# Turning attention probabilities with a transposing DMA instead of TensorE, in a one-core hybrid streaming layer

## The chip, the cores and the metric

The kernel runs on one core of a Trainium2 chip. The metric is device time in microseconds (us) of one execution. Before the change the median of three runs is 1910.07 us (1909.86 to 1910.68).

## What is computed

One layer of a streaming encoder over 1024 prompt frames and 32 sample frames, with 512 cached frames for the sample part. The part that the change touches is differential attention: eight heads, two softmax maps per head, their difference times the values.

```python
s = jnp.einsum('bqhcd,bkhcd->bhcqk', q_blk, ka).astype(jnp.float32) * scale
mask = k_chunk[None, :] <= q_chunk[:, None]
p = jax.nn.softmax(jnp.where(mask, s, -jnp.inf), axis=-1)
a = p[:, :, 0] - lam * p[:, :, 1]
return jnp.einsum('bhqk,bkhe->bqhe', a.astype(va.dtype), va)
```

Beside it run a retention branch with the same heads, an output projection, a SwiGLU block of width 2816 and a gated per-layer embedding.

## The kernel before

All matrix products of fp32 data are made from fp16 pairs: a number is scaled and split into a head ("hi") and a rest ("lo"), and a product is three fp16 matmuls (hi·hi, hi·lo, lo·hi).

The first stage, from the start to about 1050 us, is the input projection with attention and retention. Its work comes in units: 8 heads times 9 blocks of 128 rows, of which blocks 0 to 7 are the prompt and block 8 is the sample. Each unit is made twice, as `unit_a` (q, k, v and attention) and, four units later, as `unit_b` (retention, gates and the mix). Each begins with a projection of 24 matmuls of 512 columns (lines 734 to 736). Weights come by 1 MB loads on the queue of SyncE (SP), four per head, line 407. The later stages (output projection, gate and up products, down product, the gated embedding) begin behind that.

`attend` is the attention of one unit:

- TensorE makes the scores (lines 875 and 878) into a bank `sc`, one map at a time when there are more than 512 keys.
- VectorE reduces the maximum (line 885), VectorE or GpSimd scales it (line 887), ScalarE takes the exponential with the row sum (line 895) into two SBUF tiles `p` of 1024 fp32 columns. The pool has five of them.
- VectorE joins the two maps (line 909): `p0 = p0 + cz * p1`. Rows are queries, columns are keys.
- For the product with the values the keys have to lie on the partitions. Block i has i + 1 key blocks of 128 columns; the sample unit has five. TensorE turns each 128x128 fp32 block against an identity (line 924), up to four blocks into one PSUM bank `t`. ScalarE or VectorE writes the scaled fp16 head out of the bank (lines 931 and 933), VectorE the rest (line 935), both into the tile `aT` (two buffers).
- TensorE multiplies `aT` with the values (lines 943, 944, 947) into a bank `po`; ScalarE takes it out (line 956).

In all there are 8 x (1 + 2 + ... + 8 + 5) = 328 blocks to turn.

The order of the work is not written by hand. Each unit is a Python generator that announces its next step with an assumed price (`V`, `S`, `G`, `M`, `DM` for VectorE, ScalarE, GpSimd, TensorE and DMA), its waits and the buffers that it takes and gives back. `Flow` plays the generators against each other and emits the instruction that could start first. What it emits is a fixed order on each engine; on the chip an engine waits where an operand is late. `either` lets Flow choose between two engines by their assumed loads. DMAs are issued from SP in the order in which Flow reached them.

Of the kernel before, what the change touches and what calls it, by code (L numbers as in the profile page):

```python
# [11 lines left out]
F32 = mybir.dt.float32  # L12
F16 = mybir.dt.float16
BF16 = mybir.dt.bfloat16
I32 = mybir.dt.int32
AF = mybir.ActivationFunctionType
ALU = mybir.AluOpType
# [4 lines left out]
P = 128  # L22
D = 1024
# [35 lines left out]
def V(n, f=1.0, x=0.0):  # L59
    return {"V": 0.07 + x + f * n / 960.0}  # L60


def S(n, x=0.0):
    return {"S": 0.1 + x + n / 1200.0}
# [6 lines left out]
def M(us):  # L71
    return {"M": us}


def DM(mb):
    return {"D": mb * 2.9}


def either(*ds):
    out = {}  # L80
    for d in ds:
        out.update(d)
    return out
# [100 lines left out]
def kernel(  # L184
# [26 lines left out]
    nc = tc.nc  # L211
# [30 lines left out]
    id32 = cst_sb[:, 0, :]  # L242
# [245 lines left out]
    with ExitStack() as pa:  # L488
# [18 lines left out]
        lsc = ca.tile([P, 1], F32, name="lsc")  # L507
# [5 lines left out]
        wk = pa.enter_context(DT(name="wk", bufs=2))  # L513
# [3 lines left out]
        ps_o = pa.enter_context(DT(name="ps_o", bufs=3, space=PSUM))  # L517
# [346 lines left out]
        def attend(key, i, R, q4, sblocks, masked, vblocks, NK, sc_ap, do_ap):  # L864
            pm, Z = [], sm(2, "Z", 6)
            nm = sm(2, "nm", 6)
            nb = sm(2, "nb", 6)
            for ms in ((0, 1),) if NK <= 512 else ((0,), (1,)):
# [3 lines left out]
                for m in ms:  # L872
                    for b0, n, kts in sblocks:
                        o = ps[0:R, 512 * ms.index(m) + b0:512 * ms.index(m) + b0 + n]
# [11 lines left out]
                g = yield either(V(1, 1.0, 0.06), G(1, 0.2))  # L886
                ENG[g].tensor_scalar(out=nb[0:R, mc], in0=nm[0:R, mc], scalar1=sc_ap[0:R], scalar2=None, op0=ALU.mult)  # L887
                for m in ms:
                    yield ("get", "p")
                    yield S(NK, 0.14)  # L890
                    pt = pp_.tile([P, 1024], F32, tag="p", name="p")
                    if NK % P and not m:
# [13 lines left out]
                                           op0=ALU.mult, op1=ALU.mult)  # L906
            p0, p1 = pm[0][0:R, 0:NK], pm[1][0:R, 0:NK]
            yield V(NK, 1.0, 0.06)
            nc.vector.scalar_tensor_tensor(out=p0, in0=p1, scalar=cz[0:R], in1=p0, op0=ALU.mult, op1=ALU.add)
            yield ("put", "p")  # L910
            yield V(1)
            dz = sm(1, "dz", 6)
            nc.vector.tensor_tensor(out=dz[0:R], in0=rz[0:R, 0:1], in1=do_ap[0:R], op=ALU.mult)
            nb_ = len(vblocks)
            yield ("get", "aT")
            aT = wk.tile([P, 2, 8, P], F16, tag="aT", name="aT")
            for j0 in range(0, nb_, 4):
                js = range(j0, min(j0 + 4, nb_))
                yield ("get", "o")
                yield M(0.107 * len(js))  # L920
                pt = ps_o.tile([P, 512], F32, tag="o", name="t").rearrange("p (b c) -> p b c", b=4)
                for j in js:
                    n = vblocks[j][0]
                    nc.tensor.transpose(out=pt[0:n, j - j0, 0:R], in_=pm[0][0:R, j * P:j * P + n], identity=id32[0:R, 0:R])
                if js[-1] == nb_ - 1:
                    yield ("put", "p")
                n, nj = vblocks[js[-1]][0], len(js)
                hi = aT[0:n, 0, j0:j0 + nj, 0:R]
                g = yield either(S(nj * R, 0.05), V(nj * R, 1.0, 0.06))
                if g == "S":  # L930
                    nc.scalar.activation(hi, pt[0:n, 0:nj, 0:R], AF.Copy, scale=lsc[0:n])
                else:
                    nc.vector.tensor_scalar(out=hi, in0=pt[0:n, 0:nj, 0:R], scalar1=lsc[0:n], scalar2=None, op0=ALU.mult)
                yield V(nj * R, 1.0, 0.06)
                nc.vector.scalar_tensor_tensor(out=aT[0:n, 1, j0:j0 + nj, 0:R], in0=pt[0:n, 0:nj, 0:R], scalar=lsc[0:n], in1=hi,
                                               op0=ALU.mult, op1=ALU.subtract)
                yield ("put", "o")
            yield ("get", "o")
            yield M(0.165 * nb_)
            po = ps_o.tile([P, 512], F32, tag="o", name="po")[0:R, 0:P]  # L940
            for j in range(nb_):
                n, v_hi, v_lo = vblocks[j]
                nc.tensor.matmul(out=po, lhsT=aT[0:n, 0, j, 0:R], rhs=v_hi, start=(j == 0), stop=False)
                nc.tensor.matmul(out=po, lhsT=aT[0:n, 0, j, 0:R], rhs=v_lo, start=False, stop=False)
            for j in range(nb_):
                n, v_hi, v_lo = vblocks[j]
# [4 lines left out]
            if u >= NQ:  # L951
# [13 lines left out]
                                           op0=ALU.mult, op1=ALU.mult)  # L965
# [1123 lines left out]
```

## Time and profile before

| | |
|---|---|
| median of three runs | 1910.07 us |
| span of the profiled execution | 1908.6 us |
| matmuls | 14223 |
| first turn of a probability block (line 924) | at 59.6 us |
| last value product (line 947) | at 1019.0 us |
| granted TensorE clock | 0.998 |

The profiled execution's own time is its span and some 1.5 us around it, if it is taken to be the median. In the profile PE is TensorE's matmuls, PEld its weight loads, DVE is VectorE, ACT is ScalarE, POOL is GpSimd and SP is SyncE, which issues the DMAs. "L924" is line 924. A matmul row's duration runs from its start to a modelled end; matmuls overlap, so the time that one occupies the array is the distance to the next one's start. A wait line reads: who waited, for whom, us in total, times, longest.

### The profile page before, as it was taken

How to read it: one execution, taken by the hardware profiler on the slowest of the kernel's cores; microseconds unless marked ns; L12 is line 12 of the kernel's file. 1: busy time of each engine (PE TensorE's matmuls, PEld its weight loads, DVE VectorE, ACT ScalarE, POOL GpSimd, SP SyncE). 2: the span in 40 equal slices, each digit the busy share in tenths (PEclk: the TensorE clock that was granted, in tenths of full speed). 3: DMA queues.
4: the chain of work that ended last, by engine and by line, in shares of the span. 5: the costliest groups of instructions: out<-in, count | busy, mean ns of one | idle time of the engine just before them, and what ended most of it. 6: DMA issues, size and time to landing. Idle time of an engine off the chain costs nothing.

```text
span 1908.6 us, 38365 instructions
## 1 busy us (share of the span) xinstructions
PE 1859.8 (97%) x14223; PEld 1220.3 (64%) x14223; DVE 1497.7 (78%) x3940; ACT 1087.3 (57%) x2842; POOL 680.9 (36%) x1149
## 2 busy tenths in 40 slices
PE   7999999999999999999999997999999999999999
PEld 3556565555655566655556685777777776666666
DVE  7888888788787787777887589999999986654364
ACT  7777677677676776766666345655555552101132
POOL 3654444445444544544442067333232300000010
PEclk9999999999999999999999999999999999999999
DMA  5222112112021121211215610222211116112031
GB/s 194 70 72 78 60 32 82 36 55 83 24 70 58 50 64 34 79 59 31 85 33 187 226 65 31 101 86 83 69 55 66 47 54 262 61 62 79 10 133 50
DMA packets 71949, 146.90 MB, mean 77 GB/s; under 512 B 25265, under 2 KB 52145, under 8 KB 63826
## 3 DMA queue, kind: packets, MB, share of 16 engines
q1 hardware_dynamic: 71762, 144.46, 22.7%
q8 instruction: 111, 1.82, 0.4%
q14 instruction: 76, 0.62, 0.1%
HBM read 113.09 MB, written 31.34 MB: 76 GB/s over the span
## 4 chain that ended last, share of the span: by engine, by line
PE 73%; DVE 12%; POOL 7%; ACT 5%; issue 2%; DMA 1%; SPq 0%; POOLq 0%; ACTq 0%; DVEq 0%
PE ps L474 10%; PE ps L475 10%; PE ps L476 10%; PE pj L734 7%; PE pj L736 7%; PE pj L735 7%; PE ps L1478 4%; PE ps L1477 4%; PE ps L1476 4%; ACT p L895 2%; DVE nm L885 2%; DVE w L467 1%; POOL qkr L770 1%; PE sc L875 1%; PE sc L878 1%
## 5 line engine op out<-in xcount | busy, mean ns | idle before, releaser
L734 PE MATMUL pj<-w,xh 128*128 128x512 f16 x1024 | 389.0, 380 | 2.8 <-ACT w L465 2.8
L735 PE MATMUL pj<-w,xh 128*128 128x512 f16 x1024 | 389.0, 380 | 0.6 <-DVE w L467 0.6
L736 PE MATMUL pj<-w,xh 128*128 128x512 f16 x1024 | 389.0, 380 | 0.0
L475 PE MATMUL ps<-mixs,w 128*128 128x352 f16 (+1 forms) x960 | 260.4, 276 | 5.9 <-DVE mixs L1501 5.9
L474 PE MATMUL ps<-mixs,w 128*128 128x352 f16 (+1 forms) x960 | 260.4, 276 | 0.3 <-ACT pws L1354 0.3
L476 PE MATMUL ps<-mixs,w 128*128 128x352 f16 (+1 forms) x960 | 260.5, 276 | 0.0
L476 PEld LDWEIGHTS <-w 128*128 128x128 f16 x1736 | 170.4, 98 | 56.2 <-issue 6.0
L474 PEld LDWEIGHTS <-w 128*128 128x128 f16 x1736 | 170.6, 98 | 54.4 <-issue 4.4
L475 PEld LDWEIGHTS <-w 128*128 128x128 f16 x1736 | 170.4, 98 | 49.8 <-issue 1.6
L736 PEld LDWEIGHTS <-xh 128*128 128x128 f16 x1024 | 100.3, 98 | 122.3 <-issue 1.9
L1634 POOL TENSOR_TENSOR st<-st 128x512 f32<-128x512 f32 x66 | 88.2, 1336 | 244.7 <-DVE w L1629 186.6
L734 PEld LDWEIGHTS <-xh 128*128 128x128 f16 x1024 | 101.3, 99 | 76.7 <-issue 3.7
L735 PEld LDWEIGHTS <-xh 128*128 128x128 f16 x1024 | 100.2, 98 | 74.6 <-issue 3.7
L895 ACT ACTIVATE p<-sc,nb,scs 128x256 f32<-128x256 f32 (+7 forms) x128 | 106.4, 832 | 71.5 <-POOL nb L887 49.0
L474 PE MATMUL ps<-tT,w 128*128 128x352 f16 (+1 forms) x528 | 144.0, 277 | 0.0
L475 PE MATMUL ps<-tT,w 128*128 128x352 f16 (+1 forms) x528 | 143.9, 277 | 0.0
L476 PE MATMUL ps<-tT,w 128*128 128x352 f16 (+1 forms) x528 | 143.8, 277 | 0.0
L1629 DVE SCALAR_TENSOR_TENSOR w<-st,gus,w 128x512 f16<-128x512 f32 x132 | 141.4, 1072 | 0.1
L885 DVE TENSOR_REDUCE nm<-sc 128x2 f32<-128x256 f32 (+6 forms) x112 | 102.7, 917 | 19.7 <-PE sc L878 18.4
L1478 PE MATMUL ps<-a,w 128*128 128x352 f16 x312 | 97.5, 313 | 0.5 <-DVE w L1720 0.5
L1477 PE MATMUL ps<-a,w 128*128 128x352 f16 x312 | 97.5, 313 | 0.0
L1476 PE MATMUL ps<-a,w 128*128 128x352 f16 x312 | 97.5, 313 | 0.0
(432 smaller groups left out, 4861.1 us busy)
## 6 DMA issues: line engine op xcount, KB each, us to landing
st<-in_win_dram SPq DMA_DIRECT2D x30, 1024.0 KB, 4.9
st<-in_wgu_dram SPq DMA_DIRECT2D x22, 1024.0 KB, 4.8
st<-in_wdn_dram SPq DMA_DIRECT2D x16, 704.0 KB, 4.7
out_dram<-kv SPq DMA_DIRECT2D x64, 128.0 KB, 1.7
a_d<-a SPq DMA_DIRECT2D x9, 528.0 KB, 2.6
b<-a_d SPq DMA_DIRECT2D x9, 528.0 KB, 7.5
mixs<-mix_d SPq DMA_DIRECT2D x8, 528.0 KB, 6.1
pw_d<-pws SPq DMA_DIRECT2D x12, 352.0 KB, 5.3
```

What stands on the lines that cost most here:

```text
L474: nc.tensor.matmul(out=ps, lhsT=wh, rhs=ah, start=first, stop=False)
L475: nc.tensor.matmul(out=ps, lhsT=wh, rhs=al, start=False, stop=False)
L476: nc.tensor.matmul(out=ps, lhsT=wl, rhs=ah, start=False, stop=last)
L734: nc.tensor.matmul(out=ps, lhsT=xhi, rhs=w[:, k, 0], start=(k == 0), stop=False)
L735: nc.tensor.matmul(out=ps, lhsT=xhi, rhs=w[:, k, 1], start=False, stop=False)
L736: nc.tensor.matmul(out=ps, lhsT=xh[:, k, 1, t0:t0 + P], rhs=w[:, k, 0], start=False, stop=(k == KD - 1))
L885: nc.vector.tensor_reduce(out=nm[0:R, mc], in_=pv, axis=AX.X, op=ALU.max, negate=True)
L895: nc.scalar.activation(pt[0:R, 0:NK], ps[0:R, p0:p0 + NK], AF.Exp, bias=nb[0:R, m:m + 1], scale=sc_ap[0:R], accum_out=Z[0:R, m:m + 1])
L1476: nc.tensor.matmul(out=ps, lhsT=wt[:, 0, j], rhs=a[:, 0, cs], start=(first and j == js[0]), stop=False)
L1477: nc.tensor.matmul(out=ps, lhsT=wt[:, 1, j], rhs=a[:, 0, cs], start=False, stop=False)
L1478: nc.tensor.matmul(out=ps, lhsT=wt[:, 2, j], rhs=a[:, 1, cs], start=False, stop=(last and j == js[-1]))
L1629: nc.vector.scalar_tensor_tensor(out=w[:, i, 1], in0=src, scalar=s, in1=w[:, i, 0], op0=ALU.mult, op1=ALU.subtract)
```

## The change

The turn by TensorE is taken out. After the two maps are joined, head and rest are made in rows in SBUF: the second `p` tile, whose content is used up, is viewed as 2048 fp16 columns and takes the head of all key blocks and behind it the rest. Each is one instruction over all key blocks, where before there was one for each four blocks. One transposing DMA, issued from SP, then turns all of it into `aT`. The value product is as before, and waits for the DMA. In Flow the DMA has the assumed price `xbar` on the DMA resource and lands after the delay `landed`; the second `p` tile is given back when it has landed, the first as soon as the rest is made.

```diff
+def xbar(tiles):
+    return 0.5 + 0.027 * tiles
+def landed(tiles):
+    return ("delay", 2.0 + 0.03 * tiles)
...
-            yield ("put", "p")
             yield V(1)
             dz = sm(1, "dz", 6)
             nc.vector.tensor_tensor(out=dz[0:R], in0=rz[0:R, 0:1], in1=do_ap[0:R], op=ALU.mult)
             nb_ = len(vblocks)
+            NB = nb_ * P
+            pf = pm[1].bitcast(F16)
+            hi, lo, src = pf[0:R, 0:NB], pf[0:R, NB:2 * NB], pm[0][0:R, 0:NB]
+            g = yield either(S(NB, 0.05), V(NB, 1.0, 0.06))
+            if g == "S":
+                nc.scalar.activation(hi, src, AF.Copy, scale=lsc[0:R])
+            else:
+                nc.vector.tensor_scalar(out=hi, in0=src, scalar1=lsc[0:R], scalar2=None, op0=ALU.mult)
+            yield V(NB, 1.0, 0.06)
+            nc.vector.scalar_tensor_tensor(out=lo, in0=src, scalar=lsc[0:R], in1=hi, op0=ALU.mult, op1=ALU.subtract)
+            yield ("put", "p")
             yield ("get", "aT")
-            aT = wk.tile([P, 2, 8, P], F16, tag="aT", name="aT")
-            for j0 in range(0, nb_, 4):
-                js = range(j0, min(j0 + 4, nb_))
-                yield ("get", "o")
-                yield M(0.107 * len(js))
...
-                for j in js:
-                    n = vblocks[j][0]
-                    nc.tensor.transpose(out=pt[0:n, j - j0, 0:R], in_=pm[0][0:R, j * P:j * P + n], identity=id32[0:R, 0:R])
...
-                nc.vector.scalar_tensor_tensor(out=aT[0:n, 1, j0:j0 + nj, 0:R], in0=pt[0:n, 0:nj, 0:R], scalar=lsc[0:n], in1=hi,
-                                               op0=ALU.mult, op1=ALU.subtract)
-                yield ("put", "o")
+            aT = wk.tile([P, 2 * 8 * P], F16, tag="aT", name="aT")[:, 0:2 * NB].rearrange("p (a j c) -> p a j c", a=2, c=P)
+            yield X(xbar(2 * nb_ * R // 16))
+            nc.sync.dma_start_transpose(out=aT.rearrange("p a j c -> p (a j) c")[:, :, 0:R], in_=pf[0:R, 0:2 * NB])
+            yield landed(2 * nb_ * R // 16)
+            yield ("put", "p")
             yield ("get", "o")
             yield M(0.165 * nb_)
```

What moves is the order that Flow makes. The pieces below are of the eight-block unit of the fifth head. New line numbers are higher: 734 to 736 became 748 to 750, the value product's 943, 944 and 947 became 950, 951 and 954.

On TensorE before, the eight turns of this unit stand in two groups of four. This is the first, between a projection (`pj`) and the q and k turns of another unit (`qst`):

```order
L736 LDWEIGHTS xh_83
L736 MATMUL pj_9938<-w_8822,xh_83 128x512
L924 MATMUL t_9978<-cst_sb_67,p_9833 128x128 [waits DVE_49]
L924 MATMUL t_9978<-cst_sb_67,p_9833 128x128 x3
L1072 LDWEIGHTS qst_9939 [waits DVE_49]
L1072 MATMUL t_9984<-id16_88,qst_9939 128x128 [waits Activation_49]
```

Its value product begins behind that, and waits for VectorE:

```order
L735 MATMUL pj_9938<-w_8822,xh_83 128x512
L736 LDWEIGHTS xh_83
L736 MATMUL pj_9938<-w_8822,xh_83 128x512
L943 LDWEIGHTS aT_9967
L943 MATMUL po_10053<-vh_127,aT_9967 128x128 [waits DVE_49]
```

Now there is no turn on TensorE, and the same unit's value product waits for a DMA:

```order
L749 MATMUL pj_9925<-w_7696,xh_83 128x512
L750 LDWEIGHTS xh_83
L750 MATMUL pj_9925<-w_7696,xh_83 128x512
L950 LDWEIGHTS aT_9812 [waits DMAHW1_49]
L950 MATMUL po_9945<-vh_127,aT_9812 128x128
```

The first of these two products stands 38 wide (512-column) matmuls behind the unit's last score matmul, the second 76.

On VectorE before, the rest was made bank by bank, 512 columns each (L935); other units' work stands between:

```order
L935 SCALAR_TENSOR_TENSOR aT_9967<-t_9978,lsc_103,aT_9967 128x512 [waits Activation_49]
L885 TENSOR_REDUCE nm_10006<-sc_10013 128x1 [waits PE_49]
L887 TENSOR_SCALAR nb_10007<-nm_10006,csc_8641 128x1 [waits DVE_49]
L1244 SCALAR_TENSOR_TENSOR mixT_10029<-t_10024,smx_8560,mixT_10029 128x128 [waits DMAHW3_49,Activation_49]
L935 SCALAR_TENSOR_TENSOR aT_9967<-t_10018,lsc_103,aT_9967 128x512 [waits PE_49,Activation_49]
```

Now the joining (L923), head (L935, here on VectorE) and rest (L937) are each 1024 columns wide:

```order
L923 SCALAR_TENSOR_TENSOR p_9645<-p_9730,cz_9749,p_9645 128x1024 [waits DMAHW7_49,DVE_49]
L899 TENSOR_REDUCE nm_9719<-sc_9752 128x1 [waits PE_49]
L926 TENSOR_TENSOR dz_9771<-rz_9745,dop_7283 128x1
L1180 TENSOR_TENSOR S2_134<-S2_134,pr_9706 64x128
L447 TENSOR_TENSOR wamh_9775<-wam4_9636 128x1 [waits Activation_49]
L1251 SCALAR_TENSOR_TENSOR mixT_9769<-t_9757,smx_8377,mixT_9769 128x128 [waits DMAHW2_49,Activation_49]
L1182 TENSOR_SCALAR S2_134<-S2_134 64x128 [waits DVE_49]
L935 TENSOR_SCALAR p_9730<-p_9645,lsc_103 128x1024
L244 TENSOR_SCALAR B0c_9798<-mt_9796 128x1 [waits PE_49]
L937 SCALAR_TENSOR_TENSOR p_9730<-p_9645,lsc_103,p_9730 128x1024 [waits DVE_49]
```

Two passes over 512 columns became one over 1024, and seven instructions of other work stand inside the unit's chain.

On SP before, around the same unit, there are the stores of keys and values (L1049) and of the mix (L1246):

```order
L1246 DMA mix_d_65<-mixT_9790 256x1x128 [waits DMAHW3_49,DVE_49,Activation_49]
L1049 DMA out_1_dram<-kv_9823 32x256 [waits DMAHW4_49,Activation_49,Pool_49]
L1246 DMA mix_d_65<-mixT_10029 256x1x128 [waits DMAHW5_49,DVE_49]
L1049 DMA out_1_dram<-kv_10086 128x256 [waits DMAHW6_49,Activation_49,Pool_49]
L798 DMA st_10392<-in_ckT_dram 64x1024 [waits DMAHW7_49,DVE_49]
```

Now the transposing DMAs stand among them, in one queue:

```order
L1253 DMA mix_d_65<-mixT_9563 256x1x128 [waits DMAHW6_49,DVE_49]
L1056 DMA out_1_dram<-kv_9545 32x256 [waits Pool_49]
L1253 DMA mix_d_65<-mixT_9769 256x1x128 [waits DMAHW0_49,DVE_49]
L942 DMA_TRANSPOSE aT_9812<-p_9730 128x16x128 [waits DMAHW1_49,DMAHW3_49,DVE_49,PE_49]
L1253 DMA mix_d_65<-mixT_9884 256x1x128 [waits DMAHW2_49,DVE_49]
```

There are 72 of them, one per unit; an eight-block unit's covers 128x16x128 fp16, which is 512 KB.

More of the change, by code (lines that the diff above doesn't have):

```diff
@@ L76, in DM, with X @@
     return {"D": mb * 2.9}
+def X(us):
+    return {"D": us}
+def xbar(tiles):
+    return 0.5 + 0.027 * tiles
+def landed(tiles):
+    return ("delay", 2.0 + 0.03 * tiles)
 def either(*ds):
@@ L914, in attend @@
             nb_ = len(vblocks)
-            yield ("get", "aT")
-            aT = wk.tile([P, 2, 8, P], F16, tag="aT", name="aT")
-            for j0 in range(0, nb_, 4):
-                js = range(j0, min(j0 + 4, nb_))
-                yield ("get", "o")
-                yield M(0.107 * len(js))
-                pt = ps_o.tile([P, 512], F32, tag="o", name="t").rearrange("p (b c) -> p b c", b=4)
-                for j in js:
-                    n = vblocks[j][0]
[L924 to L935, printed above, removed]
-                                               op0=ALU.mult, op1=ALU.subtract)
-                yield ("put", "o")
```

## The prediction

> **What bounds the kernel now.** I read the page's busy shares first, then its chain.
>
> ```profile
> span 1908.6 us, 38365 instructions
> PE 1859.8 (97%) x14223; PEld 1220.3 (64%) x14223; DVE 1497.7 (78%) x3940; ACT 1087.3 (57%) x2842; POOL 680.9 (36%) x1149
> PE 73%; DVE 12%; POOL 7%; ACT 5%; issue 2%; DMA 1%; SPq 0%; POOLq 0%; ACTq 0%; DVEq 0%
> ```
>
> TensorE carries most of the chain. The change lies between 59.6 and 1019.0 us, so I asked for the busy times of just that stretch.
>
> ```profile
> core 0: us, PE busy (x) PEld busy (x) DVE busy (x) ACT busy (x) POOL busy (x), PEclk, DMA share, GB/s
> 60.00:1020.00 960.00, 946.58 (x6990) 566.04 (x6989) 781.14 (x2397) 669.46 (x1991) 453.64 (x921) 1.00 0.18 56
> ```
>
> PE has 13 us without a matmul in 960, DVE 179, ACT 291, and the DMA engines are 18% busy. A busy PE is not yet a full one, since matmul rows overlap. So I looked at single starts in the timeline of PE, around four turns.
>
> ```profile
> start us, us, engine line op out<-in xcount [idle before <-releaser]
> 507.22 0.38 PE L735 MATMUL pj<-w,xh 128*128 128x512 f16 x1
> 507.44 0.38 PE L736 MATMUL pj<-w,xh 128*128 128x512 f16 x1
> 507.65 0.60 PE L924 MATMUL t<-cst_sb,p 128*128 128x128 f32 x4
> 508.09 0.39 PE L1163 MATMUL por<-vr,inn 128*128 128x128 f32 x2
> 508.31 0.38 PE L875 MATMUL sc<-kcs,q 128*128 128x512 f16 x1
> 508.53 0.38 PE L878 MATMUL sc<-kcs,q 128*128 128x512 f16 x1
> ```
>
> A wide matmul starts 0.22 us after the one before though its row lasts 0.38. The starts have no holes, and the four turns take 508.09 - 507.65 = 0.44 us, 0.11 us each. What PE does not have to issue here is time won, as long as nothing else comes late. The waits of PE in the same stretch are small:
>
> ```profile
> PE t L924 <- DVE p L909: 1.5, 3, 1.0
> PE po L943 <- DVE aT L935: 1.1, 3, 0.4
> ```
>
> PE waits 1.1 us in all for the operand `aT` of the value product, over 72 units. The planned order and the chip agree that closely, and that is what the change puts at stake.
>
> **The change part by part.**
>
> *Turns leave TensorE.* The group row gives their number:
>
> ```profile
> L924 PE MATMUL t<-cst_sb,p 128*128 128x128 f32 x328 | 54.8, 275 | 3.1 <-DVE p L909 1.5 <-DVE aT L935 0.8 <-ACT of L956 0.4
> ```
>
> 328 x 0.11 = 36.1 us, all on the path, since PE is full. (The row's 54.8 us counts overlapping ends.) The 3.1 us of idle before them is not credited; it falls on whatever stands next.
>
> *Head and rest.* Before and now, in groups:
>
> ```profile
> L935 DVE SCALAR_TENSOR_TENSOR aT<-t,lsc,aT 128x512 f16<-128x512 f32 (+2 forms) x112 | 67.2, 600 | 8.6 <-ACT aT L931 8.1
> L909 DVE SCALAR_TENSOR_TENSOR p<-p,cz 128x128 f32<-128x128 f32 (+8 forms) x72 | 59.1, 821 | 1.0
> L931 ACT ACTIVATE aT<-t,lsc 128x512 f16<-128x512 f32 (+3 forms) x69 | 40.1, 581 | 44.3 <-PE t L924 39.0 <-PE mt L816 5.0
> L933 DVE TENSOR_SCALAR aT<-t,lsc 128x512 f16<-128x512 f32 (+2 forms) x43 | 25.3, 588 | 4.9 <-PE t L924 4.8
> ```
>
> The rest becomes 72 instructions of the widths of L909 (the sample's a little wider), which read SBUF as it does: about 60 us for 67.2 on DVE. The head keeps its columns, now 28 on DVE and 44 on ACT in the order; from 65.4 us together it loses some fixed cost of 40 instructions. With 179 and 291 us free in the stretch both stay beside PE: no gain and no loss on the path. Were that cover gone (DVE full), the 7 us would count; it is far from that.
>
> *The transposing DMA.* No transposing DMA is in the trace, so its price is bounded by what plain ones take and by what the order leaves. What the order leaves, for an eight-block unit: from its last score matmul to its value product there now stand 76 wide matmuls (76 x 0.215 = 16.3 us), 12 fp32 ones (at the turn's 0.11, 1.3) and a few narrow ones (0.4): 18.0 us. It was 38 wide ones, 17 fp32 ones (its own eight turns among them) and 27 narrow ones. In that time its own chain runs:
>
> ```profile
> L885 DVE TENSOR_REDUCE nm<-sc 128x1 f32<-128x1024 f32 x16 | 19.5, 1217 | 1.8 <-PE sc L878 1.8
> L887 POOL TENSOR_SCALAR nb<-nm,scs 128x1 f32<-128x1 f32 x46 | 26.5, 577 | 89.9 <-DVE nm L885 85.8 <-DVE A1c L230 3.2
> L895 ACT ACTIVATE p<-sc,nb,scs 128x1024 f32<-128x1024 f32 x16 | 19.2, 1203 | 16.5 <-DVE nb L887 10.6 <-POOL nb L887 5.9
> L909 DVE SCALAR_TENSOR_TENSOR p<-p,cz 128x1024 f32<-128x1024 f32 x7 | 9.0, 1285 | 0.2
> ```
>
> Maximum 1.22, scaling 0.58, exponential 1.20, joining 1.29, then head and rest of the same width, 1.2 and 1.29: 6.8 us. Seven instructions of other work stand inside it on DVE (a reduction of 544 columns and small ones), an estimated 2 us. About 9 us are left for the DMA. The nearest rows to it are plain DMAs:
>
> ```profile
> w<-in_xN_dram SPq DMA_DIRECT2D x8, 512.0 KB, 4.4
> b<-a_d SPq DMA_DIRECT2D x9, 528.0 KB, 7.5
> mix_d<-mixT SPq DMA_DIRECT2D x64, 64.0 KB, 2.0
> out_dram<-kv SPq DMA_DIRECT2D x8, 32.0 KB, 1.5
> st<-in_win_dram SPq DMA_DIRECT2D x30, 1024.0 KB, 4.9
> ```
>
> 512 KB land in 4.4 us from issue, at most 7.5 in a crowd; 64 KB, the one-block unit, in 2.0. The planner's own assumption for 128 tiles is 0.5 + 3.5 + 2.0 + 3.8 = 9.8 us, for 16 tiles 3.4. So the order puts the value product just where the assumed DMA ends, and a DMA that costs up to twice a copy still lands in time. I take the lower half of that range, 4.4 to 9 us: a turned transfer is bytes moved in small pieces, which is nearest to the copies, and the assumption on top covers twice that. Cost on PE then: nothing, but for crowding. 30 weight loads of 1 MB hold the DMA engines some 4.9 - 2.0 = 2.9 us each, 9% of the 960 us; a turn that falls behind one is late by half that: 72 x 0.09 x 1.45 = 9.4 us. The planner spreads them, so this is an upper value; I keep it for all small waits of this kind.
>
> A rule speaks against this change: the Trainium skill, "VectorE: DVE Perf Modes", section "The three transpose paths", gives 1309 ns for a 128x128 block by the DMA crossbar and 390 ns by TensorE, and its rules say to use TensorE if PSUM will do. Here TensorE's turn takes 0.11 us of PE's time, not 390 ns, so by the trace the change can win even less than that page would have it. What the DMA's figure would make of the time is the second rival below. Another page, "Advanced Engine Details and Errata", section "X-Bar Transpose (TRN2)", has transposes at about 90% of a copy's rate, an estimated 4.9 us for 512 KB, and the sum would stand as it is.
>
> *SP's queue.* The DMAs of keys, values and mix, and the loads, now queue with 72 turns, and a turn queues behind them. The waits of SP's queue say whether its order fits:
>
> ```profile
> SPq L1049 <- POOL kv L1048: 262.6, 55, 7.3
> ```
>
> SP waits for the data, not the data for SP: 55 of 72 stores were at the head before they were ready. A store or mix takes 0.3 to 0.5 us to issue. Loads behind a turn come some us later, and they are made units ahead. I cost this at nothing.
>
> *Longer chain.* A unit now holds its second `p` tile and its `aT` until the DMA lands and the product runs, 5 to 6 us longer. With 960 / 72 = 13.3 us a unit, five `p` tiles at two a unit come round after 33 us and two `aT` after 27, so this is covered too. Values of the next head overwrite those that the last prompt unit reads, and that product is later now: within the 9.4 us.
>
> **Sum.** -36.1 + 9.4 = -26.7 us. On the profiled execution, 1908.6 + 1.5 of span and surroundings: 1883.4; the same on the median of 1910.07. I forecast 1883 us. With no new wait it is 1874, with the 3.1 us of old idle gone too, 1871.
>
> **The rivals.**
>
> *The turn lands later than its place in the order (slower).* Place: the value product's first weight load, in each unit. Eighteen us of order against 13.3 us a unit means that the next unit's scores are mostly issued before the stall, so part of it helps the next: I count 13.3 / 18.0 = 0.74 of each, 72 x 0.74 = 53 us of time for each us of lateness. It decides from 36 / 53 = 0.7 us on. At 1.5 us late: +80 - 36 = 44, 1954 us. For it: the order leaves hardly more than the code's assumption, and SP's own work to issue a transposing DMA is shown nowhere. Against: copies need half. Chance 0.19.
>
> *The turn goes block by block (slower by far).* If the crossbar takes one 128x128 block (32 KB) after the other, each at the nearest row's 1.5 us, an eight-block unit's 16 blocks of head and rest need 24 us where 9 are left. The mean unit has 656 / 72 = 9.1 blocks, or 73 tiles, for which the order leaves what the code assumes, 0.5 + 2.0 + 2.0 + 2.2 = 6.7 us; they need 13.7, so each unit is 7.0 late: 53 x 7.0 - 36 = +335, 2245 us. By the 1309 ns of the Trainium skill's page "VectorE: DVE Perf Modes" the estimate is 5.2 us late and some 2150 us. The row of 32 KB is mostly a fixed latency that would not repeat in one DMA, which speaks against. Chance 0.08.
>
> *The gain is eaten up (no change).* Turns 0.6 to 0.8 us late on the mean: 1906 to 1914. Chance 0.07.
>
> *A smaller gain.* Late by 0.4 to 0.6 us, 1895 to 1906: chance 0.06.
>
> **How the numbers follow.** The forecast and its neighbourhood, 1868 to 1895, have 0.60. A measurement of this kernel can tell about 0.2%, some 4 us, from no change. Faster: 0.60 + 0.06 = 0.66; same 0.07; slower 0.19 + 0.08 = 0.27. The range must reach into the slow side to leave out at most 0.2: 1868 to 1955, which leaves out the block-by-block case and the worse half of the late one. The likeliest case's own range is 1868 to 1895.
>
> **What would show it.** Right: no L924; the first value product of a unit (L950) waits for `aT` by DMA in few units and under 10 us in all; the DMA of 512 KB lands in under 9 us; last value product near 993 us. Wrong: a wait of PE on DMA `aT` that comes back in every unit, PE's busy time in the stretch below 95%, SP's queue with turns that stand behind others. If PE waits on something else, on ACT or DVE, then the sum failed at the cover, not at the DMA.

## The result and the profile after

The changed kernel takes 1899.89 us (median of four runs, 1899.07 to 1900.08) against 1910.2 us for the kernel before on the same chip: ratio 0.9945, 95% interval 0.9933 to 0.9957. It is 10.3 us faster; 27 were forecast. The runs of each kernel in this document agree within 0.3%, but for one slow run of `e18_act_truer` (4911.6 us), which its median leaves out. The page:

```profile
span 1898.0 us, 37821 instructions
PE 1830.6 (96%) x13895; PEld 1181.9 (62%) x13895; DVE 1492.4 (79%) x3872; ACT 1083.4 (57%) x2828; POOL 702.5 (37%) x1151
PE 68%; DVE 14%; POOL 7%; ACT 6%; issue 3%; DMA 2%; SPq 0%; POOLq 0%; DVEq 0%; ACTq 0%
```

All 328 turns are gone from TensorE (14223 matmuls, now 13895). But its share of the chain fell from 73% to 68%: other engines now end waits more often. The same stretch as in the prediction, in which more of the later work now lies:

```profile
core 0: us, PE busy (x) PEld busy (x) DVE busy (x) ACT busy (x) POOL busy (x), PEclk, DMA share, GB/s
60.00:1020.00 960.00, 934.53 (x6846) 541.23 (x6847) 783.02 (x2361) 678.07 (x2010) 480.71 (x937) 1.00 0.32 85
```

PE has 25 us without a matmul there, where it had 13. The operand that the prediction feared for is not what it waits on. The transposing DMA in the view of its tile, with the durations on SP's queue and then the times to landing:

```profile
L942 SPq DMA_TRANSPOSE aT<-p x72: 1174/1336/2533, 60.8 to 999.1; - x72
DMA to landing us min/median/max: 2.3/3.5/5.6
```

It lands in 2.3 to 5.6 us, quicker than the planner assumed (3.4 to 9.8). The 5.6 is not the largest size: the eight-block units, 512 KB, land in 4.3 to 4.6 us. TensorE's waits from 60 to 1003 us, the largest rows and that of the DMA:

```profile
PE t L1244 <- DVE mx L1239: 4.7, 5, 1.7
PE sc L889 <- ACT p L909: 3.4, 7, 0.9
PE pr L1162 <- ACT qT L402: 3.2, 6, 0.9
PE sc L889 <- DVE q L402: 1.8, 3, 0.9
PE por L1170 <- DVE inn L1168: 1.8, 4, 1.1
...
PE po L950 <- DMA aT<-p: 1.1, 2, 0.8
```

All rows of this answer make 23 us, where the kernel before has 11. They are many and small, on steps that the change did not touch: the mix, the scores, the retention. Head and rest, in groups of that stretch:

```profile
L937 DVE SCALAR_TENSOR_TENSOR p<-p,lsc 128x640 f16<-128x640 f32 (+7 forms) x72 | 60.3, 837 | 2.3 <-ACT p L933 2.0
L933 ACT ACTIVATE p<-p,lsc 128x256 f16<-128x256 f32 (+7 forms) x43 | 32.7, 761 | 12.2 <-DVE p L923 10.5 <-DVE hdB L1135 1.4 <-POOL oss L783 0.2
L935 DVE TENSOR_SCALAR p<-p,lsc 128x640 f16<-128x640 f32 (+6 forms) x28 | 15.9, 568 | 0.0
```

The rest costs 60.3 us, as worked out, and the head 48.6, where at most 65.4 was counted.

The second loss is at the end of the stage. TensorE's last projection starts at 1003.4 us, 22.3 earlier than before (1025.7). Behind the projections it makes the products of the gated embedding (`pj<-w`), then the output projection (`ps<-mixs,w`). Before, one followed the other:

```profile
1052.86 0.31 PE L476 MATMUL pj<-w 128*128 128x352 f16 x1
1053.10 0.38 PE L286 MATMUL mt<-o1mc,cst_sb 1*128 1x1 f32 x2
1053.81 0.31 PE L474 MATMUL ps<-mixs,w 128*128 128x352 f16 x1 [0.34 <-ACT pws L1354]
```

Now (start, duration, and in brackets the idle time with what ended it):

```profile
1030.94 0.31 PE L490 MATMUL pj<-w 128*128 128x352 f16 x1
1038.31 0.37 PE L289 MATMUL mt<-cst_sb,wam 128*1 128x128 f32 x1 [7.06 <-DVE wam L449]
1039.68 0.58 PE L300 MATMUL mt<-o0mc,cst_sb 1*128 1x1 f32 x2 [1.00 <-DVE o0mc L292]
...
1041.77 0.47 PE L488 MATMUL ps<-mixs,w 128*128 128x352 f16 x1 [0.25 <-DVE o1c L244]
```

The `mt` rows spread the maxima of the third and fourth block of the output weights over the partitions; TensorE's order has them ahead of the first output product. What they wait for stands on VectorE and on SP's queue:

```profile
1028.61 2.46 DVE L440 TENSOR_REDUCE wam<-st 128x2 f32<-128x512 f32 x4
1036.83 0.69 DVE L440 TENSOR_REDUCE wam<-st 128x2 f32<-128x512 f32 x1 [5.77 <-DMA st<-in_wo_dram]
```

```profile
1028.72 0.34 SPq L421 DMA_DIRECT2D st<-in_wo_dram  x1
```

The fourth block is loaded at 1028.7, when the second has been split out of the same staging buffer, and lands 8 us later. VectorE's order has a reduction of the fourth block ahead of the last step of the third, so both wait for that load. The output projection starts 12.0 us earlier than before, not 22.3, and what follows takes 856.2 us against 854.8. So the 36 us of turns became 22, then 12, then 10.

### The profile page after: what moved, and what is told of

The parts are those of the page before. It is cut to its first block, busy times and chain, and to the rows that moved or that the text cites. A ratio compares the mean times of both kernels' runs of the same rounds, so it can differ in the third digit from the quotient of the medians.

```text
span 1898.0 us, 37821 instructions
## 1 busy us (share of the span) xinstructions
PE 1830.6 (96%) x13895; PEld 1181.9 (62%) x13895; DVE 1492.4 (79%) x3872; ACT 1083.4 (57%) x2828; POOL 702.5 (37%) x1151
## 2 busy tenths in 40 slices
DMA packets 158220, 168.38 MB, mean 89 GB/s; under 512 B 111537, under 2 KB 138417, under 8 KB 150098
## 4 chain that ended last, share of the span: by engine, by line
PE 68%; DVE 14%; POOL 7%; ACT 6%; issue 3%; DMA 2%; SPq 0%; POOLq 0%; DVEq 0%; ACTq 0%
PE ps L488 9%; PE ps L489 9%; PE ps L490 9%; PE pj L748 7%; PE pj L750 7%; PE pj L749 7%; PE ps L1485 4%; PE ps L1484 4%; PE ps L1483 4%; ACT p L909 2%; DVE nm L899 1%; PE sc L889 1%; POOL qkr L784 1%; DVE w L1636 1%; PE sc L892 1%
## 5 line engine op out<-in xcount | busy, mean ns | idle before, releaser
L899 DVE TENSOR_REDUCE nm<-sc 128x1 f32<-128x896 f32 (+6 forms) x112 | 102.8, 918 | 11.1 <-PE sc L892 10.3
```

Source lines behind the costliest of these rows:

```text
L899: nc.vector.tensor_reduce(out=nm[0:R, mc], in_=pv, axis=AX.X, op=ALU.max, negate=True)
```

## The experiments

Times are medians; the ratio is to the kernel before on the same chip. The two starts, in us, are read off the trace: the last projection (end of the units) and the first output product (end of the stage).

| kernel | us | ratio, 95% interval | last projection | first output product |
|---|---|---|---|---|
| before | 1910.2 | 1 | 1025.7 | 1053.8 |
| changed | 1899.9 | 0.9945, 0.9933 to 0.9957 | 1003.4 | 1041.8 |
| e1_price | 1902.4 | 0.9957, 0.9945 to 0.9970 | 1016.1 | 1046.1 |
| e2_copy | 1900.3 | 0.9946, 0.9933 to 0.9958 | 1002.5 | 1039.5 |
| e3_wo | 1894.0 | 0.9915, 0.9902 to 0.9929 | 1006.8 | 1036.3 |
| e4_half | 1896.8 | 0.9932, 0.9918 to 0.9946 | 1011.5 | 1039.9 |
| e5_hold | 1893.8 | 0.9912, 0.9899 to 0.9926 | 1002.5 | 1032.2 |
| e6_cover | 1892.8 | 0.9906, 0.9893 to 0.9920 | 999.8 | 1036.0 |
| e7_act | 1897.0 | 0.9929, 0.9916 to 0.9941 | 1007.3 | 1041.8 |
| e8_pieces | 1906.9 | 0.9982, 0.9973 to 0.9991 | 1009.1 | 1047.6 |
| e9_margin | 1883.4 | 0.9859, 0.9846 to 0.9873 | 995.7 | 1027.5 |
| e10_truer | 1880.7 | 0.9844, 0.9830 to 0.9857 | 991.5 | 1021.2 |
| e11_before_margin | 1901.5 | 0.9953, 0.9941 to 0.9966 | 1017.3 | 1044.7 |
| e12_before_truer | 1896.8 | 0.9928, 0.9915 to 0.9942 | 1012.8 | 1041.1 |
| e13_truer_only | 1883.2 | 0.9857, 0.9843 to 0.9872 | 992.0 | 1025.2 |
| e14_truer_margin | 1882.4 | 0.9854, 0.9838 to 0.9871 | 991.8 | 1026.2 |
| e15_cover_truer | 1868.6 | 0.9783, 0.9769 to 0.9798 | 984.5 | 1013.4 |
| e16_dearer | 1881.4 | 0.9848, 0.9833 to 0.9863 | 983.8 | 1012.1 |
| e17_nodma_truer | 1869.5 | 0.9787, 0.9772 to 0.9801 | 981.4 | 1014.4 |
| e18_act_truer | 1881.9 | 0.9853, 0.9833 to 0.9873 | 994.8 | 1025.1 |

**e1_price: the DMA at its measured price.**

```diff
-    return 0.5 + 0.027 * tiles
+    return 0.4 + 0.007 * tiles
...
-    return ("delay", 2.0 + 0.03 * tiles)
+    return ("delay", 1.6 + 0.02 * tiles)
```

> The changed kernel with the order made from lower prices: occupied 0.4 + 0.007 us and landing 1.6 + 0.02 us per tile, which gives 2.6 us for 16 tiles and 5.7 for 128, where the trace of the changed kernel has 2.3 and 5.6 from issue to landing (assumed before: 3.4 and 9.8). Theory A (the order was made for too slow a DMA, so value products stand too late and p and aT are held too long): the 14 us that TensorE lost in the units come back in good part, 1888 to 1893 us, ratio to the kernel before 0.988 to 0.991. Rivals (the loss is at the end of the stage, or in the traffic, or in other engines' lateness): within 3 us of 1900, ratio 0.993 to 0.996, first output product still near 1040 us.

1902.4 us, and a last projection 12.7 us later than in the changed kernel: theory A falls. The order now puts the value product where the DMA just lands, and TensorE waits for it:

```profile
PE po L950 <- DMA aT<-p: 8.0, 9, 2.4
```

So the too high price had been a margin, at least in part: these waits are 6.9 of the 12.7 us. The new price of an eight-block unit, 5.7 us, was read off the longest landing; these units in fact land in 4.3 to 4.6.

**e2_copy: the same bytes without turning.**

```diff
-            nc.sync.dma_start_transpose(out=aT.rearrange("p a j c -> p (a j) c")[:, :, 0:R], in_=pf[0:R, 0:2 * NB])
+            nc.sync.dma_start(out=aT.rearrange("p a j c -> p (a j) c"), in_=pf[:, 0:2 * NB])
```

> The changed kernel with the transposing DMA replaced by a plain DMA of the same bytes from the same tile to the same tile, so the value product multiplies blocks that are not turned. The order of TensorE, VectorE, ScalarE and GpSimd is the same. Theory B (the traffic costs it: the 86000 more packets slow other engines' accesses and other transfers, GpSimd's equal instructions took 15.7 us more and VectorE's 11.1): GpSimd's and VectorE's durations fall back and the time falls to 1885 to 1890, ratio 0.987 to 0.990. Rivals: the packets fall to about 80000 but the time stays within 3 us of 1900, ratio 0.993 to 0.996, and GpSimd stays slower.

```profile
DMA packets 82316, 168.38 MB, mean 89 GB/s; under 512 B 26417, under 2 KB 56369, under 8 KB 74194
```

The packets fall from 158220 to 82316, and the median landing from 3.5 to 2.5 us. The time does not move, and GpSimd's equal instructions (those of the same names and shapes in both kernels, 60 to 1020 us) still take 15.4 us more than before. Theory B falls: neither the packets nor the turning cost anything in this order. The bytes are the same in both, so this does not test them.

**e3_wo: the output weights ahead of the units.**

```diff
-                        flow.add(load_wo_0(), 1)
+                        flow.add(load_wo_0(), -3)
```

> The changed kernel with one number changed: the first two blocks of the output projection's weights are made at priority -3, not 1, so their maxima and splits go ahead of the units' work on VectorE and ScalarE when both are ready. Theory C (10 of the 22 us that the last projection is earlier are lost at the end of the stage, because TensorE's order has the maximum of the fourth weight block ahead of the first output product, and that block comes last through two buffers): the fourth block is loaded by 1015 instead of 1028.7, the first output product starts at 1031 to 1034 us instead of 1041.8, time 1890 to 1893, ratio 0.989 to 0.991. Rival (DVE and ACT are full there, what the weights gain the units lose): first output product 1038 or later, 1896 to 1901.

The fourth block is loaded at 1019.2, and the first output product starts at 1036.3, 2.7 us behind the last embedding product instead of 10.9. The units pay 3.4 us for it. 5.9 us are won in all: theory C holds, though the start and the time lie 2.3 and 1.0 us beyond its ranges, and so does part of its rival.

**e5_hold: the fourth block out of TensorE's way.** The block's load stays; maxima, spreading (there in the bank `ss`), scale and split are one generator `held_block` of the next stage.

```diff
+        if hold is not None:
+            hold.update(st=st, out=out)
+            return
         norm = rowf is None and not tail
...
-                flow.add(split_block(wos[1][0], 1, tail["hold"]["st"], None, tail["hold"]["sk"]), 0)
+                flow.add(held_block(wos[1][0], 1, mixun, tail["hold"]["st"], wos[1][1]), 0)
...
+                        if (c, m) == (0, 6):
+                            yield ("wait", "wo3")
```

> The changed kernel with one step of the stage's end moved: the fourth block of the output projection's weights is loaded where it was, but its maxima, their spreading over TensorE and its scaling are announced in the next stage, beside the first output products, which do not need it. The units' order stays. Theory C (at the stage's end TensorE's order makes the first output product wait for the fourth block): TensorE's 7.1 us wait at the spreading goes, the first output product starts 0.5 to 2 us behind the last product of the gated embedding, near 1032 instead of 1041.8, time 1889 to 1892, ratio 0.989 to 0.991. Rival (the mix of the last head, loaded in the crowd, or the third block is as late): first output product 1038 or later, 1896 to 1900.

```profile
1031.29 0.31 PE L509 MATMUL pj<-w 128*128 128x352 f16 x1
1031.53 0.38 PE L300 MATMUL mt<-o0mc,cst_sb 1*128 1x1 f32 x2
1032.25 0.31 PE L507 MATMUL ps<-mixs,w 128*128 128x352 f16 x1 [0.34 <-ACT pws L1380]
```

The wait is gone and the output projection starts 9.6 us earlier. Of these, 3.6 are lost behind it (859.8 us instead of 856.2). 1893.8 us: the end of the stage was worth 6.1 us, not 10.

**e4_half and e6_cover: less for TensorE, without the change.** e4 makes each group of turns one bf16 matmul, which does not turn the blocks; e6 leaves the third part of the value product out as well.

```diff
-                yield M(0.107 * len(js))
+                yield M(0.054 * len(js))
...
+                nc.tensor.matmul(out=pt[:, 0:len(js), :].rearrange("p b c -> p (b c)"), lhsT=top[0],
+                                 rhs=top[1][:, j0 * P:(j0 + len(js)) * P], start=True, stop=True)
...
-                nc.tensor.matmul(out=po, lhsT=aT[0:n, 1, j, 0:R], rhs=v_hi, start=False, stop=(j == nb_ - 1))
```

> The kernel before with the turns cheaper on TensorE and nothing else changed: each group of up to four fp32 turns becomes one bf16 matmul of the group's columns (bf16 heads of the probabilities against the identity), so the blocks are not turned and the value product multiplies others. No DMA is added, head and rest are made from the bank as before. A wide matmul takes 0.215 us for four blocks where four turns took 0.44, so TensorE has 328 x 0.11 - 328 x 0.054 = 18 us less to issue. Theory D (the cover is thin: what is taken from TensorE is in part given back by waits on VectorE, ScalarE and GpSimd, with any edit): 6 to 10 us less than the kernel before, ratio 0.995 to 0.997. Rivals (the loss belongs to the DMA or to head and rest in SBUF): 15 to 18 us less, ratio 0.990 to 0.992.

> The kernel before with as much taken from TensorE as the change takes, but no DMA and head and rest from the bank as before: each group of up to four fp32 turns becomes one bf16 matmul (not turned), and the value product's third part, rest times value head, is left out. Removed: 328 x (0.11 - 0.057) + 328 x 0.056 = 36 us. Theory D (thin cover: with 36 us less on TensorE the other engines' lateness shows, whatever the way): the last projection starts 22 to 25 us earlier than before, as with the change. Theory E (what is given back belongs to head and rest made in SBUF, whose instructions are longer and beside which GpSimd's equal instructions took 15.7 us more, and to the longer chain): 29 to 33 us earlier, near 995 instead of 1003.4. The whole time then hangs on the stage's end as well: by D 1896 to 1900, by E 1883 to 1892.

e4's last projection is 14.2 us earlier for some 17 taken away (the bf16 matmul takes 0.057 us a block), e6's 25.9 for 36. That lies between the theories: 10 of 36 us come back without the DMA and without head and rest in SBUF (D), where the changed kernel lost 14. The 10 are thin cover; the 4 on top are the change's own, in these orders.

The wait view alone does not show the 10: its rows make 11.2 us before and 14.1 in e6. It counts idle time behind the end of the last row, and a wide row lasts 0.38 us where the next one can start after 0.22, so each late start costs up to 0.16 us that the view does not count. If all that the distances of starts exceed the median distance of their shape is summed, from 60 us to the last projection, TensorE loses an estimated 26.7 us before, 35.8 in e6 and 40.6 in the changed kernel. So what comes back, 9 and 14 us, is late operands.

**e7_act and e8_pieces: where and how long head and rest are.** e7 takes the choice of VectorE away; e8 makes both in a loop over pieces of 512 columns.

```diff
-            g = yield either(S(NB, 0.05), V(NB, 1.0, 0.06))
+            g = yield S(NB, 0.05)
...
+            for c0 in range(0, NB, 512):
+                cw = slice(c0, min(c0 + 512, NB))
```

> The changed kernel with the head always on ScalarE, where the order had 28 of 72 on VectorE. Theory F (VectorE's head instructions from SBUF to SBUF run at about twice the rate of its others, 0.68 us for 896 columns where the rest takes 1.17, and slow GpSimd beside them): GpSimd's equal instructions fall back from 15.7 us more than before to under 6, the last projection starts by 999 instead of 1003.4, 1893 to 1896 us. Rival (GpSimd is slowed by the other SBUF instructions or does not matter): last projection 1002 or later, 1897 to 1903.

> The changed kernel with head and rest made in pieces of at most 512 columns, as before the change, in place of one instruction over up to 1024; 112 + 112 instructions again, one DMA per unit as in the change. Theory G (single instructions of up to 1.3 us on VectorE and ScalarE hold up short urgent ones, such as the masked scores, the mix or the exponential for the score bank): TensorE's waits up to 1003 us fall from 24 us to under 17, last projection 995 to 999, 1892 to 1896 us. Rival (the length is not it; 40 instructions more cost their fixed parts): last projection 1002 to 1005, 1898 to 1904.

In e7 GpSimd's equal instructions are still 12.6 us above before and the last projection is later, 1007.3: theory F falls, though the whole is 2.9 us faster and that was not explained. In e8 waits rise to 26 us and the time to 1906.9: theory G falls. By then five orders of the changed kernel, equal within 3 us by the planner's count, had their last projection at 1003.4, 1016.1, 1006.8, 1007.3 and 1009.1. So the chip's departure from the order was the thing to test.

**e9_margin, e11_before_margin, e10_truer, e12_before_truer: orders that allow for lateness.** e9 and e10 build on e5_hold, e11 and e12 on the kernel before.

```diff
-MARGIN = 0.3
+MARGIN = 0.5
...
-    return {"V": 0.07 + x + f * n / 960.0}
+    return {"V": 1.05 * (0.07 + x + f * n / 960.0)}
...
-    return {"G": 0.15 + x + 0.0021 * n}
+    return {"G": 1.1 * (0.15 + x + 0.0021 * n)}
```

> The kernel of e5_hold with one number of the planner changed: MARGIN 0.5 in place of 0.3, the time that a TensorE step is kept back behind its operand from another engine. By the planner's own count the last projection starts at 968.6 against 965.8. Theory H (the 13 us lost in the units are lateness of other engines against an order that allows them little): TensorE's waits in 60 to 1000 us fall from 22 us to under 15, last projection 992 to 999 against 1002.5 in e5_hold, 1886 to 1891 us, ratio 0.987 to 0.990. Rival (margins do not help, the order just moves): last projection 1002 to 1008, 1893 to 1898.

> The kernel of e5_hold with the planner's prices of VectorE times 1.05 and of GpSimd times 1.1: in the trace of the changed kernel VectorE is busy 783 us where the planner counted 744 for the stage, GpSimd 481 where it counted 438, ScalarE 678 against 672. Theory H: an order made from truer prices waits less, waits under 15 us in 60 to 1000 us, last projection 992 to 999, 1886 to 1891 us. Rival (the lateness comes from single jams that no mean price shows): waits 20 us or more, 1892 to 1900.

> The kernel before with MARGIN 0.5 in place of 0.3, nothing else: what the margin is worth without the change. By the planner's count its last projection starts 3.6 us earlier. If the lateness that the margin takes away comes with the change: 1906 to 1910 us, ratio 0.998 to 1.000. If the margin helps any order by as much: 1898 to 1904, ratio 0.994 to 0.997.

> The kernel before with the planner's prices of VectorE times 1.05 and of GpSimd times 1.1: what truer prices are worth without the change. If the lateness that they take away comes with the change: 1908 to 1912 us, ratio 0.999 to 1.001. If they help any order: 1899 to 1905.

Theory H holds, in time beyond its numbers: 10.4 us from the margin, 13.1 from the prices, on top of e5_hold. TensorE's waits from 60 to 1000 us fall from 22.3 to 12.2 with the prices, and with the margin to 17.1, more than the 15 expected. But the kernel before gains 8.9 and 13.7 us in the same way: the lateness did not come with the change. e10_truer, 1880.7 us, is faster than both kernels.

**e13_truer_only to e16_dearer: the change on truer prices.** e13 is the changed kernel with e10's two lines, e14 is e10 with `MARGIN = 0.5`, e15 is e6 with e10's two lines, e16 is e10 with 1.08 and 1.15 for 1.05 and 1.1.

> The changed kernel with the planner's prices of VectorE times 1.05 and of GpSimd times 1.1, and nothing else: beside e12_before_truer (1896.75 us) it is the same change on an order from truer prices. If the loss came from the prices: last projection 21 us earlier than e12's 1012.8, near 991.5, time 1880 to 1886 us, a gain of the change of 11 to 17 us, held down by the stage's end. If it belongs to the change itself: last projection 1000 or later, 1888 or more.

> The kernel of e10_truer (stage's end mended, truer prices) with MARGIN 0.5 too. The planner's count has its last projection at 971.4 against 967.2. If lateness is left that margin takes away: TensorE's waits in 60 to 1000 us under 8 (12.2 in e10_truer) and 1874 to 1880 us. If truer prices have taken it away already: the planner's 4 us are lost, 1881 to 1887.

> The kernel of e6_cover (the kernel before with 36 us less on TensorE, no DMA, blocks not turned and the third part of the value product left out) with truer prices, VectorE times 1.05 and GpSimd times 1.1. If what e6_cover gave back (10 of 36 us) was the prices' fault: last projection 30 to 36 us earlier than e12_before_truer's 1012.8, 977 to 983. If it is a thin cover as such: 22 to 28 us earlier, 985 to 991, as with the change under the same prices.

> The kernel of e10_truer with the prices raised further, VectorE times 1.08 and GpSimd times 1.15. The planner's count has its last projection at 971.3 against 967.2. If prices are what counts: waits of TensorE in 60 to 1000 us 6 to 14, last projection 988 to 996, 1877 to 1885 us. If e10_truer was a lucky order: waits near 20 again, last projection 1000 or later, 1888 to 1896.

e16 and e14 are as fast as e10 within their intervals: truer prices help in more than one order, and more margin brings nothing. But e16 is not the same as e10 inside. Its last projection starts at 983.8, 7.7 us earlier than e10's and earlier than expected, and these 7.7 us are lost behind the first output product (867.6 us instead of 859.9). There TensorE waits 16 times for the maxima of weight blocks, 6.9 us in all from 1100 to 1560 us, where e10 has one such wait of 1.9. e13 against e12 gives the change's worth on a good order: 13.6 us, of 20.8 at the last projection. e15 against e12 gives what the same cut gives without the DMA: 28.1 us, of 28.3 at the last projection. So thin cover keeps 8 of 36 us on a good order too (28.3 lies just outside the range for it, 22 to 28), and the changed kernel keeps 7.5 more in the units, in this pair of orders. The stretch from 60 to 980 us of e12, e13 and e15 (PE busy comes first behind the length):

```profile
60.00:980.00 920.00, 917.82 (x6832) 552.99 (x6831) 757.09 (x2322) 659.20 (x1948) 436.43 (x887) 1.00 0.19 58
```

```profile
60.00:980.00 920.00, 907.08 (x6615) 528.65 (x6613) 755.85 (x2298) 663.94 (x1970) 465.90 (x913) 1.00 0.32 80
```

```profile
60.00:980.00 920.00, 912.22 (x6473) 524.33 (x6471) 789.00 (x2424) 666.53 (x1980) 452.58 (x908) 1.00 0.19 59
```

TensorE stands empty for 2.2, 12.9 and 7.8 us. Part of e13's is the transposing DMA after all, in one place:

```profile
PE po L950 <- DMA aT<-p: 4.9, 3, 4.1
```

```profile
768.15 0.38 SPq L421 DMA_DIRECT2D st<-in_win_dram  x1
768.64 1.91 SPq L942 DMA_TRANSPOSE aT<-p  x1
```

The turn goes out 0.5 us behind a weight load of 1 MB and lands 6.9 us later, the longest of this kernel. That is the crowding of the prediction. It costs more than the 4.1 us of waiting, since TensorE's granted clock is halved behind it (the column behind POOL's count), and a wide matmul starts 0.43 us after the one before:

```profile
774.70:781.50 6.80, 5.91 (x54) 4.28 (x55) 2.26 (x8) 2.24 (x9) 2.31 (x6) 0.50 0.47 169
```

```profile
779.14 0.63 PE L749 MATMUL pj<-w,xh 128*128 128x512 f16 x1
779.57 0.63 PE L750 MATMUL pj<-w,xh 128*128 128x512 f16 x1
```

TensorE works at that clock from 775.6 to 781.5 us, which is an estimated 3 us more. One late turn has cost some 7 us.

**e17_nodma_truer and e18_act_truer: which part of the change.** Both build on e13; e18 is e7's edit. e17:

```diff
+            yield ("get", "aT")
+            pf = wk.tile([P, 2 * 8 * P], F16, tag="aT", name="aT")
...
-            yield X(xbar(2 * nb_ * R // 16))
-            nc.sync.dma_start_transpose(out=aT.rearrange("p a j c -> p (a j) c")[:, :, 0:R], in_=pf[0:R, 0:2 * NB])
-            yield landed(2 * nb_ * R // 16)
```

> The kernel of e13_truer_only without its transposing DMA: head and rest are written from SBUF straight into aT, not turned, and the value product follows them at once, with the sample unit's products over 32 rows. If the DMA (its landing behind loads, p and aT held longer) takes the 7.5 us: last projection 983 to 986 us as in e15_cover_truer, 1868 to 1873 us. If head and rest from SBUF take it (longer instructions, GpSimd slower beside them): last projection 990 to 994, 1879 to 1884.

> The kernel of e13_truer_only with the head always on ScalarE. If VectorE's heads from SBUF, which slow GpSimd, take part of the 7.5 us: last projection 985 to 989, 1877 to 1881 us. If not: 990 to 996, 1881 to 1886.

Without the DMA, with head and rest in SBUF:

```profile
60.00:980.00 920.00, 915.60 (x6718) 533.25 (x6717) 765.72 (x2331) 677.21 (x1998) 461.04 (x909) 1.00 0.19 59
```

4.4 us are empty; the last projection comes at 981.4, even 3.1 us ahead of e15, and the whole takes 1869.5 us. GpSimd's equal instructions are still 16.6 us slower than in e12 (8.9 in e15, which has neither the DMA nor head and rest in SBUF), and that costs nothing here. e18 is the same as e13 within its interval. So head and rest in SBUF are free, and between e13 and e17 the DMA step costs 10.6 us in the units and 13.7 in all. That is the difference of two orders and not a price: e16, with all 72 transposing DMAs, has its last projection at 983.8, only 2.4 us behind e17, and e18, without e13's late turn, at 994.8.

## Why the prediction was wrong

- **Turns leave TensorE, -36.1 us:** the count and the price hold; not every us taken from a full PE is won. On orders of the old prices 25.9 of 36 reach the last projection when nothing else is added, on truer ones 28.3. I read PE's small waits (1 to 2 us a row) as proof of cover. They said how the other engines kept up with a TensorE that had 36 us more to do, and nothing of how they would with less.
- **Head and rest, nothing:** right, by e17, and so is the working (109 us in the two groups).
- **The transposing DMA of 512 KB lands in 4.4 to 9 us:** right at its lower edge, 4.3 to 4.6. Both slow rivals fall with it: no late turn in every unit, and a further block costs an estimated 0.14 us and not 1.5.
- **The failed step, "all on the path, since PE is full":** the sum took the 36.1 us to the end of the kernel, less 9.4. The runs show 25.5 coming back in place of 9.4: 13.8 in the units (36.1 - 22.3), 10.3 at the end of the stage and 1.4 behind it.
- **In the units, "I keep it for all small waits of this kind":** 9.4 lies near 13.8 by luck. It was worked out for turns that land late behind weight loads, and on the old prices TensorE waits 1.1 us for the DMA in all; e13 has one such place. The larger part is thin cover, 10 us, for which the sum had no term. What the change adds to that is 3.6 us on the old prices (25.9 against 22.3) and 7.5 or 10.6 on the truer ones (against e15 and e17), so it is no fixed price. Of the 10.6, 4.9 are waits on the DMA itself and some 3 the halved clock behind the longest; whether the rest comes from later value products, from longer held `p` and `aT` or from the order alone was not separated.
- **The end of the stage, which the sum left out:** I ended at the last value product and did not ask what stands behind it. This is the larger miss, 11.7 of the 16.1 us between forecast and result (26.7 and 10.6). 10.3 us were lost there between the last projection and the first output product; e5_hold shows that mending the order there brings 6.1 back. It belongs to the order and not to the DMA: e1_price, with the same 72 DMAs, takes 30.0 us from the last projection to the first output product, the kernel before 28.1, the changed kernel 38.4.
- **SP's queue, nothing:** right in that turns and stores cost no wait that comes back, though a turn takes 1.2 to 2.5 us to issue and a plain copy of the same tiles 0.5 to 0.6; e13's one long landing was issued right behind a load.
- **The signs:** the wait on `aT` and the landing came out as said, the last value product did not (993 said, 1007.6 measured). Before, it came 6.7 us ahead of the last projection; now it comes 4.2 us behind it. "If PE waits on something else, on ACT or DVE, then the sum failed at the cover" is the case that came.

In the account of the whole: 36.1 us taken from TensorE, less 10.2 by thin cover, 3.6 by the change's own part in the units, 10.3 at the end of the stage and 1.4 behind it, leaves 10.6, the difference of the two spans. Thin cover and the change's part are told apart by e6_cover alone; orders of the changed kernel differ by more than 3.6 us among themselves, so on the old prices only their sum, 13.8, is firm. Of the 10.3, e5_hold shows 6 to be recoverable.

## What to carry to other kernels

When work is taken off a full engine in a statically ordered kernel, expect not all of it back: here 72 to 87% of 36 us reached the last projection where no DMA step was added (e6, e15, e17), since every other engine's lateness shows once there is less work to hide it. Follow the gain past the last changed instruction to the end of the stage, and look there for what is ordered ahead of the next stage's first work. Compare the planner's busy time of each engine with the trace first: correcting two prices by 5 and 10% was worth more here (13.7 us without the change) than the change itself (10.3). And do not take the difference of two orders for the price of a step: orders of the changed kernel on truer prices had their last projection from 983.8 to 994.8 us.

## What the runs showed of the hardware

If the landings of the changed kernel are sorted by the width of the rest made just before, a transposing DMA from SBUF to SBUF lands in 2.30 us at the least for two 128x128 fp16 blocks (64 KB) and in 4.26 for sixteen (512 KB). Each further block takes an estimated (4.26 - 2.30) / 14 = 0.14 us. The plain copy of the same tiles in e2_copy has 1.82 and 2.93, an estimated 0.08 a block. Some landings are longer, up to 5.6 us here (a six-block unit) and 10.0 in e14_truer_margin, where TensorE waited 7.0 us for two of them; the one of 6.9 us in e13_truer_only was issued right behind a load. The Trainium skill, "VectorE: DVE Perf Modes", section "The three transpose paths", gives 1309 ns for such a block by this way. As a price of each block of one DMA the trace does not bear it out: fourteen further blocks take 2 us together.

After the 11 us at the stage's end in which TensorE had almost no matmul, its granted clock was halved for some us. The windows show it in the column behind POOL's count:

```profile
1036.00:1041.00 5.00, 1.32 (x5) 0.72 (x5) 3.66 (x14) 0.00 (x0) 0.00 (x0) 0.50 1.06 388
1041.00:1046.00 5.00, 4.75 (x21) 2.82 (x22) 4.78 (x19) 4.56 (x12) 0.00 (x0) 0.62 1.08 357
1046.00:1051.00 5.00, 5.00 (x35) 3.26 (x34) 3.32 (x8) 2.43 (x6) 0.00 (x0) 1.00 0.33 102
```

The first ten matmuls of the output projection start 0.29 us apart instead of 0.15, so the long wait costs a further 1.5 us behind itself. That is about the 1.4 us that the account has behind the stage. The Trainium skill, "TensorE: Matmul & The Clock Gate", section "Part 1: The HAM clock gate", has half rate after an idle window of about 3.4 us, and as long of sustained work until full rate returns; the trace agrees roughly, with 3 us of slow matmuls here and 6 in e13_truer_only.
